# An encoder block on one core: the beginning ordered by hand with all loads ahead of the stores, norm weights spread by transpositions, TensorE and GpSimd by hand in branch B, meta keys as one block

## Chip, core and metric

The kernel runs on one core of a Trainium2 chip. Its time is the device time in microseconds (us) of one execution. Engines: PE (TensorE), PEld (its weight loads), DVE (VectorE), ACT (ScalarE), POOL (GpSimd), SP (the engine that issues the DMAs).

## What is computed

1024 tokens of width 1024, with 16 meta tokens put ahead, go through one block; all is fp32.

```python
h = concat(meta, x)                                  # 1040 x 1024
proj = rms_norm(h, norm_mix) @ w_in                  # qa, ka, va, qb, kb, vb, gates
y_a = differential_attention(qa, ka, va)             # branch A: 4 heads of 2 x 64, all keys
y_b = windowed_gqa(qb, kb, vb, sink)                 # branch B: 8 heads, 2 groups of 4; keys of
                                                     # the own block of 128, both neighbours, meta
h = h + (sigmoid(ga) * (y_a @ w_ba) + sigmoid(gb) * (y_b @ w_bb)) @ w_o
h = h + (silu(f @ w_gate) * (f @ w_up)) @ w_down     # f = rms_norm(h, norm_ffn)
out = rms_norm(h, norm_final)[16:]
```

## The kernel before

Every fp32 operand is split in two fp32r tiles, hi and lo (`split`, L117 on ACT for hi, L118 on POOL or DVE for lo), and every product is three matmuls: hi·hi, hi·lo, lo·hi.

**Beginning.** Nine tiles of tokens (eight of 128, one of 16 meta tokens) are loaded (L383), squared on ACT (L134), given their factor on POOL (L122, L123), scaled by it and by the norm weights `gmix` on DVE (L140, `xn_a`), transposed on PE (L148, `ptn_a`) and split (L150, L151) into `hT_hi`, `hT_lo`, the transposed activations. `gmix` comes as a broadcast transfer of 128x1024 (L415). Warm-up matmuls on zeros (`idle`, L413, L426) stand ahead. Between the tiles, `advance` puts projection steps (L214; one step is the three matmuls of one of 8 row blocks) of KB and of two column blocks of QB, in chunks of 256 tokens. Their results are spread into `kb` and `qb` by 72 DMAs on SP (L282, L285, L305).

**Branch B.** VB is projected and transposed. There are 16 units, g = 0, 1 by t = 0 to 7. A unit has for each of its four heads r two score matmuls (`bps`, L331), on DVE bias and minimum (L333), on ACT the exponential (L337); then the sink's exponential (L339), denominators on DVE (L340, L341), four normalisations on POOL (L343), and a POOL copy `bmd` (L347) of the meta keys' probabilities, padded to 128 columns per head. `finish` transposes each block of keys, four heads each (L356, `bpt`), the meta block as a fourth one, splits the result (L358 ACT, L360 DVE, `btr`) and multiplies it with the values (L362, `bpy`); L365 to L367 store it. Units at the edges have two blocks of keys (288 columns), the others three (432). Beside the units with g = 0 run the projections of branch A's heads 0 and 1 (`project_a`: QA, VA, KA) and, on POOL, the token sums (L525 to L539, split on ACT and DVE as `to`); beside g = 1 heads 2 and 3 and the weight sums (L608 to L611).

**Order.** The scheduler orders each engine's queue by a simulated timeline, except inside `tc.manual_schedule`, where an engine keeps the order of the code. Before, POOL is by hand from the second QB projection on, PE from branch A on (L883). Branch A (`aps`, L796), gate products (`pg`, L717, L737), output projection, FFN (`pg`, L1293; `pd`, L1387) follow.

## Time and profile before

| | us |
|---|---|
| median of three runs | 1449.07 (1446.01, 1449.07, 1449.72) |
| the profiled execution | 1446.1 |
| its span, first to last instruction | 1444.3 |
| PE busy | 1422.8 |
| DVE, ACT, POOL busy | 899.2, 679.6, 641.3 |

Rows give the start or the stretch, the duration, the engine, the line and the tiles. Busy PE counts each matmul to its modelled end, which overlaps the start of the next.

### The profile page before, as it was taken

To read this page: it belongs to the slowest core of one execution; us is meant where nothing else is said; L and a number is where in the kernel's file an instruction comes from. 1 tells how busy PE (TensorE), PEld (TensorE's weight loads), DVE (VectorE), ACT (ScalarE), POOL (GpSimd) and SP (SyncE) were. 2 spreads that over 40 slices of the span, in tenths; PEclk is the share of its full clock that TensorE was granted. 3 is DMA by queue.
4 is the path that set the end of the run, shared out by engine and by line. 5 is a ranking of instruction groups with operands and counts; after the bars stand their busy time and mean duration, and the time that the engine had idled before them with its cause. 6 is when DMAs were issued, how large, how long until landed. Compare 5 with 4: busy or idle time off the path is not lost.

```text
span 1444.3 us, 21160 instructions
## 1 busy us (share of the span) xinstructions
PE 1422.8 (99%) x7279; PEld 1221.2 (85%) x7279; DVE 899.2 (62%) x1624; ACT 679.6 (47%) x1290; POOL 641.3 (44%) x605
## 2 busy tenths in 40 slices
...
GB/s 244 90 209 237 193 162 265 288 281 213 190 169 257 147 227 125 190 256 209 216 34 88 152 104 161 109 102 110 102 102 96 110 102 102 331 208 140 124 129 139
DMA packets 188891, 242.41 MB, mean 168 GB/s; under 512 B 18208, under 2 KB 115936, under 8 KB 188784
## 3 DMA queue, kind: packets, MB, share of 16 engines
...
q8 instruction: 57, 0.93, 0.3%
q14 instruction: 50, 0.41, 0.1%
...
## 4 chain that ended last, share of the span: by engine, by line
PE 81%; POOL 6%; DVE 5%; issue 4%; DMA 2%; ACT 1%; POOLq 0%; SPq 0%; DVEq 0%; ACTq 0%
PE pg L1293 28%; PE pd L1387 9%; PE pg L737 7%; PE po L1070 6%; PE ppa L780 6%; PE aps L796 3%; PE pp_qb L214 3%; POOL oa L118 3%; PE apy L835 3%; PE pp_ka L214 2%; PE pp_va L214 2%; PE apt L822 2%; PE pp_qa L214 2%; PE bpt L356 1%; PE bpy L362 1%
## 5 line engine op out<-in xcount | busy, mean ns | idle before, releaser
L118 POOL TENSOR_TENSOR wop<-wf,wop 128x512 fp32r<-128x512 f32 x128 | 172.6, 1353 | 165.5 <-ACT wop L117 149.6
L1293 PE MATMUL pg<-t,wop 128*128 128x512 f32 x1056 | 242.6, 389 | 0.0
L1293 PEld LDWEIGHTS pg<-t,wop 128*128 128x128 f32 x1056 | 198.3, 188 | 41.1
L1387 PE MATMUL pd<-ob,oa 128*128 128x512 f32 x924 | 209.9, 389 | 0.4 <-POOL oa L118 0.4
L1387 PEld LDWEIGHTS pd<-ob,oa 128*128 128x128 f32 x924 | 173.4, 188 | 36.8 <-POOL oa L118 0.8
L1293 PE MATMUL pg<-b,wop 128*128 128x512 f32 x792 | 185.6, 392 | 2.3 <-DVE c L1302 2.3
L1293 PEld LDWEIGHTS pg<-b,wop 128*128 128x128 f32 x792 | 149.5, 189 | 34.1 <-issue 2.4
L737 PE MATMUL pg<-hT_hi,gop 128*128 128x512 f32 x384 | 142.7, 396 | 0.0
L118 POOL TENSOR_TENSOR oa<-ra,oa 128x512 fp32r<-128x512 f32 x33 | 44.0, 1335 | 170.1 <-ACT oa L117 168.6
L117 ACT ACTIVATE wop<-wf 128x512 fp32r<-128x512 f32 x128 | 80.2, 631 | 82.9 <-PE pg L1293 48.6
L118 POOL TENSOR_TENSOR gop<-gr,gop 128x512 fp32r<-128x512 f32 x48 | 63.3, 1319 | 116.4 <-ACT gop L117 102.6
L117 ACT ACTIVATE oa<-ra 128x512 fp32r<-128x512 f32 x77 | 48.7, 632 | 105.9 <-PE pd L1387 45.1
L804 ACT ACTIVATE as<-as,amn 128x1040 f32<-128x1040 f32 x64 | 74.5, 1164 | 46.9 <-DVE amn L799 42.8
L1128 DVE TENSOR_TENSOR s<-wf,wf 128x512 f32<-128x512 f32 x22 | 25.0, 1138 | 108.1 <-DMA wf<-in_w_ff_gate_dram 58.0
L796 PE MATMUL aps<-ak,aq 128*128 128x392 f32 (+1 forms) x384 | 90.0, 330 | 1.3 <-DVE amn L799 0.6
L1070 PE MATMUL po<-woh,mT 128*128 128x512 f32 x384 | 88.0, 390 | 0.0
L1070 PEld LDWEIGHTS po<-woh,mT 128*128 128x128 f32 x384 | 71.9, 188 | 14.8
L796 PEld LDWEIGHTS aps<-ak,aq 128*128 128x128 f32 x384 | 69.6, 189 | 15.0 <-DVE amn L799 2.2
L737 PEld LDWEIGHTS pg<-hT_hi,gop 128*128 128x128 f32 x384 | 72.7, 189 | 11.2 <-DVE gk L742 0.2
L343 POOL TENSOR_SCALAR bs<-bs,bdn 128x432 f32<-128x432 f32 (+1 forms) x64 | 41.4, 666 | 85.5 <-DVE bdn L341 73.4
L737 PE MATMUL pg<-hT_lo,gop 128*128 128x512 f32 x192 | 76.0, 396 | 0.0
L807 POOL TENSOR_SCALAR as<-as,adn,neglam 128x1040 f32<-128x1040 f32 x32 | 38.8, 1214 | 62.5 <-DVE adn L805 43.9
...
## 6 DMA issues: line engine op xcount, KB each, us to landing
...
```

The source lines that it names most:

```text
L117: nc.scalar.activation(hi, src, AF.Copy)
L118: lo_eng.tensor_tensor(lo, src, f32(hi), ALU.subtract)
L214: nc.tensor.matmul(ps[:, :n], a[:, c, :], b[:, c, at:at + n], start=(c == 0 and i == 0), stop=(c == DC - 1 and i == 2))
L343: nc.gpsimd.tensor_scalar(st[:, r, :W], st[:, r, :W], dn[:, r:r + 1], 1.0, ALU.mult, ALU.mult)
L737: nc.tensor.matmul(ps, op[:, a, c], quad(b, *act)[:, c], start=(p in (2, 5, 1) and c == 0 and i == 0), stop=(p in (2, 3, 4) and c == 3 and ...
L780: nc.tensor.matmul(ps, w[:, a, j, :], src(j, b, tk), start=(j == 0 and n == 0), stop=(j == 3 and n == 2))
L796: nc.tensor.matmul(ps[:, :n], qs[m][:, t * P:(t + 1) * P], ks[m][:, vv, k0:k0 + n], start=(vv == 0), stop=(vv == 1))
L804: nc.scalar.activation(s[m][:, 0:L], s[m][:, 0:L], AF.Exp, bias=low, scale=-1.0, accum_out=dn[:, m:m + 1])
L835: nc.tensor.matmul(py[:, cols], v[:kp, a, k, :], at_[:kp, k, b, :], start=(k == 0 and j == 0), stop=(k == 8))
L1070: nc.tensor.matmul(ps, mT[:, c, a, t * P:(t + 1) * P], wos[q, c][:, b], start=(c == 0 and n == 0), stop=(c == DC - 1 and n == 2))
L1293: nc.tensor.matmul(ps, op[:, x, c, :], b[:, y, c, :], start=(p in (1, 2, 5) and c == 0 and n == 0), stop=(p in (4, 2, 3) and c == 3 and n ...
L1387: nc.tensor.matmul(ps[u], oa[:, a, u * P:(u + 1) * P], ob[:, b, :], start=(p in (1, 2, 5) and j == 0 and k == 0), stop=(p in (2, 3, 4) and ...
```

## The change

- **Beginning.** All engines keep the order of the code until tile 6 is turned. The loads of x and of the weights of KB and QB are issued before the first store. The norm weights come as 8x128, are transposed, and eight transposes of a broadcast column build `gmix`. Warm-ups are 24 instead of 22. The first two KB chunks multiply all hi·hi first, then hi·lo, then lo·hi.
- **Branch B.** PE (from VB on) and POOL keep the order of the code. A unit is cut in two generators, `scores()` (a step per head; the last also issues the normalisation) and `turns()` (meta transpose and first block; a block each; values and store). `plan` hangs them on projection steps: scores at base-14, -12, -10, -8, turns at base, +4, +8, +12, with base = 16t+4 for g = 0 and 182+13t for g = 1; a piece of the token sums every 8 steps.
- **Meta keys.** The probabilities of four heads by 32 columns (each meta key twice) are one 128x128 block with one transpose. Four ACT copies and four DVE subtractions put it block-diagonally into `diag`, against values with the meta rows repeated eight times.
- **Small.** One tile for the small loads; `vb1` allocated later; one Silu activation after the merging, so that the table is loaded there.

PE around unit 2 of g = 0 (`bps_2_3` are its last scores; `va`, `qa` are branch A's projections; `bpt_2_8` the meta transpose). Before:

```order
L331 MATMUL bps_2_3_1103<-kb_146,qb_156 128x432 x2
L362 MATMUL bpy_0_1053<-btr_0_0_1059,vb_148 128x512
...
L356 MATMUL bpt_1_8_1151<-ident,bmd_151 128x128 x3
L356 MATMUL bpt_2_1_1198<-ident,bs_2_1087 128x128 x4
...
L356 MATMUL bpt_2_8_1228<-ident,bmd_150 128x128 x2
L362 MATMUL bpy_2_1197<-btr_2_3_1223,vb_148 128x512
```

70 rows lie between the scores and the unit's first transposes, and 140 between them and the meta transposes. Now, on the same engine:

```order
L348 MATMUL bps_2_3_1316<-kb_146,qb_149 128x432 x2
L225 MATMUL pp_va_384_1288<-hT_hi,wh_c_1063 128x384
...
L381 MATMUL bpy_1_1224<-btr_1_2_1311,vb_148 128x512 x2
L399 MATMUL bpy_1_1224<-diag,vb_148 128x512
L225 MATMUL pp_va_768_1358<-hT_hi,wh_c_1063 128x272
...
L385 MATMUL bpt_2_8_1372<-ident,bmd_2_1329 128x128
L374 MATMUL bpt_2_1_1376<-ident,bs_2_1257 128x128 x4
```

The meta transpose comes first of the transposes, behind 12 matmuls of 384 columns (four steps), three `bpy` and 12 of 272.

ACT at the same unit (`to` are splits of token sums, which POOL computes; `bes` the sink's exponentials). Before:

```order
L337 ACTIVATE bs_2_1087,bdn_2_1089<-bs_2_1087,bmn_2_1088 128x432
L117 ACTIVATE to_1_1619<-ta_1_1614 128x512
L337 ACTIVATE bs_2_1087,bdn_2_1089<-bs_2_1087,bmn_2_1088 128x432 x2
L339 ACTIVATE bes_2_1090<-bes_2_1090 128x4
L358 ACTIVATE btr_0_8_1079<-bpt_0_8_1074 128x512
```

Now:

```order
L117 ACTIVATE to_0_1186<-ta_0_1181 128x512
L352 ACTIVATE bs_2_1257,bdn_2_1259<-bs_2_1257,bmn_2_1258 128x432 x2
L376 ACTIVATE btr_1_2_1311<-bpt_1_2_1306 128x512
L352 ACTIVATE bs_2_1257,bdn_2_1259<-bs_2_1257,bmn_2_1258 128x432
L117 ACTIVATE to_0_1250<-ta_0_1182 128x512
L357 ACTIVATE bes_2_1260<-bes_2_1260 128x4
```

A second `to` stands between the last exponential and that of the sink.

The beginning on SP. Before:

```order
L383 DMA x_185<-in_x_dram 128x1024
L415 DMA gmix<-in_norm_mix_dram 128x1024
L383 DMA x_188<-in_x_dram 128x1024
L180 DMA w_c_190<-in_w_in_dram 128x8x128
L383 DMA x_203<-in_x_dram 128x1024
```

Now:

```order
L459 DMA g_168<-in_norm_mix_dram 8x128
L421 DMA x_170<-in_x_dram 128x1024
L421 DMA x_172<-in_x_dram 128x1024
L178 DMA w_174<-in_w_in_dram 128x8x128
L178 DMA w_176<-in_w_in_dram 128x8x128
L421 DMA x_178<-in_x_dram 128x1024
```

The norm weights are 4 KB instead of 512 KB and stand ahead of tile 0. The diff, cut to its core:

```diff
+            dots = [(c, i) for c in range(DC) for i in range(3)]
+            if name == "kb" and at < 512:
+                dots.sort(key=lambda d: d[1])
             for c in range(DC):
-                for i, (a, b) in enumerate(terms):
-                    nc.tensor.matmul(ps[:, :n], a[:, c, :], b[:, c, at:at + n],
-                                     start=(c == 0 and i == 0), stop=(c == DC - 1 and i == 2))
+                for d, i in dots[3 * c:3 * c + 3]:
+                    a, b = terms[i]
+                    nc.tensor.matmul(ps[:, :n], a[:, d, :], b[:, d, at:at + n],
+                                     start=((d, i) == dots[0]), stop=((d, i) == dots[-1]))
...
+        meta = vt[:, S:S + 2 * NM]
+        if name == "vb":
+            meta = bpool.tile([P, P], F32, tag="by1", name="vb_meta", bufs=2)
+            nc.vector.tensor_copy(meta.rearrange("p (a k) -> p a k", a=8), vt[:, S:L].unsqueeze(1).broadcast_to([P, 8, NM]))
...
+            for r in range(4):
+                ps = bank(psum1, "bs", f"bps_{nm}_{r}", 2)
+                for v in range(2):
+                    nc.tensor.matmul(ps[:, :W], qb[:, r, t * P:(t + 1) * P],
+                                     kb[g][:, v, b0:b1, :].rearrange("p b k -> p (b k)"), start=(v == 0), stop=(v == 1))
+                nc.vector.tensor_tensor_reduce(st[:, r, :W], ps[:, :W], tb, 2.0 ** -(4 * g + r + 1), nsink[:, 4 * g + r:4 * g + r + 1],
+                                               ALU.add, ALU.min, mn[:, r:r + 1])
+                nc.scalar.activation(st[:, r, :W], st[:, r, :W], AF.Exp, bias=mn[:, r:r + 1], scale=-1.0,
+                                     accum_out=dn[:, r:r + 1])
+                if r < 3:
+                    yield
+            nc.vector.tensor_tensor(es, mn, sinkb[:, 4 * g:4 * g + 4], ALU.add)
+            nc.scalar.activation(es, es, AF.Exp)
+            nc.vector.tensor_tensor(dn, dn, es, ALU.add)
+            nc.vector.reciprocal(dn, dn)
+            for r in range(4):
+                nc.gpsimd.tensor_scalar(st[:, r, :W], st[:, r, :W], dn[:, r:r + 1], 1.0, ALU.mult, ALU.mult)
+            md = held["md"] = bpool.tile([P, 4, 2, NM], F32, tag="bmd", name=f"bmd_{nm}", bufs=2)
+            nc.gpsimd.tensor_copy(md, st[:, :, own:own + NM].unsqueeze(2).broadcast_to([P, 4, 2, NM]))
+            yield
+
+        def turns():
+            st, md, dg, trs = held["st"], held["md"], diag[:, t % 2], {}
             py = bank(psum1, "by", f"bpy_{nm}", 1)
-            blocks = [(k, P, (k - b0) * 144) for k in range(b0, b1)] + [(8, P, (t - b0) * 144 + P)]
-            for k, kp, o in blocks:
+
+            def turn(k):
+                o = (k - b0) * 144
                 pt = bank(psum1, "bt", f"bpt_{nm}_{k}", 2).rearrange("p (r t) -> p r t", r=4)
                 for r in range(4):
-                    nc.tensor.transpose(pt[:kp, r, :], st[:, r, o:o + P] if k < 8 else md[:, r], ident)
-                tr = bpool.tile([P, 2, 4, P], F32R, tag="btr", name=f"btr_{nm}_{k}", bufs=4)
-                nc.scalar.activation(tr[:kp, 0], pt[:kp], AF.Copy)
-                lo = tr[:, 1] if k < 8 else tr[:NM, 0]
-                nc.vector.tensor_tensor(lo, pt[:lo.shape[0]], f32(tr[:lo.shape[0], 0]), ALU.subtract)
-                for hl in range(2 if k < 8 else 1):
-                    nc.tensor.matmul(py, vb[g][:kp, k, :], tr[:kp, hl].rearrange("p r t -> p (r t)"),
-                                     start=(k == b0 and hl == 0), stop=(k == 8))
+                    nc.tensor.transpose(pt[:, r, :], st[:, r, o:o + P], ident)
+                tr = trs[k] = bpool.tile([P, 2, 4, P], F32R, tag="btr", name=f"btr_{nm}_{k}", bufs=4)
+                nc.scalar.activation(tr[:, 0], pt, AF.Copy)
+                nc.vector.tensor_tensor(tr[:, 1], pt, f32(tr[:, 0]), ALU.subtract)
+
+            def value(k):
+                for hl in range(2):
+                    nc.tensor.matmul(py, vb[g][:, k, :], trs[k][:, hl].rearrange("p r t -> p (r t)"),
+                                     start=(k == b0 and hl == 0), stop=False)
+
+            pt = bank(psum1, "bt", f"bpt_{nm}_8", 2)[:, 0:P]
+            nc.tensor.transpose(pt, md.rearrange("p r a k -> p (r a k)"), ident)
+            sc = bpool.tile([P, P], F32, tag="bsc", name=f"bsc_{nm}", bufs=2)
+            nc.scalar.copy(sc, pt)
+            turn(b0)
+            for r in range(4):
+                hi, lo = slice(32 * r, 32 * r + 32), slice(32 * r, 32 * r + NM)
+                nc.scalar.activation(dg[hi, r], sc[hi], AF.Copy)
+                nc.vector.tensor_tensor(dg[lo, r], sc[lo], f32(dg[lo, r]), ALU.subtract)
+            yield
+            for k in range(b0 + 1, b1):
+                turn(k)
+                value(k - 1)
+                yield
+            value(b1 - 1)
+            nc.tensor.matmul(py, vb[g][:, 8, :], dg.rearrange("p r t -> p (r t)"), start=False, stop=True)
             y1 = bpool.tile([64, 512], F32, tag="by1", name=f"by1_{nm}", bufs=2)
             nc.scalar.copy(y1, py[64:128])
             nc.vector.tensor_tensor(y1, py[0:64], y1, ALU.add)
             nc.sync.dma_start(yb_d[g][:, t * P:(t + 1) * P].rearrange("(r p) s -> p r s", p=64),
                               y1.rearrange("p (r s) -> p r s", r=4))
-        return finish
+            yield
+
+        return scores(), turns()
...
+    xpool, close_xpool = pool("xpool", "right")
+    order_0 = tc.manual_schedule()
+    order_0.__enter__()
     zeros = bpool.tile([P, 512], BF16, tag="by1", name="zeros", bufs=2)
     nc.vector.memset(zeros, 0.0)
     idle = bank(psum1, "by", "idle", 1)
-    for _ in range(15):
-        nc.tensor.matmul(idle, zeros[:, 0:P], zeros, start=True, stop=True)
+
+    def warm(n):
+        for _ in range(n):
+            nc.tensor.matmul(idle, zeros[:, 0:P], zeros, start=True, stop=True)
+
+    g8 = bpool.tile([8, P], F32, tag="by1", name="g8", bufs=2)
+    nc.sync.dma_start(g8, norm_mix.rearrange("o (k d) -> (o k) d", k=8))
     load_x(0)
-    nc.sync.dma_start(gmix, norm_mix.broadcast_to([P, D]))
     load_x(1)
+    ask(C_KB)
+    ask(C_QB)
+    load_x(2)
+    ask(C_QB + P, bpool)
+    load_x(3)
+    for t in (4, 5, 6):
+        load_x(t, xpool)
+    warm(6)
+    gt8 = small.tile([P, 8], F32, name="gt8", bufs=1)
+    pt8 = pp_bank("pt_g8")[:, 0:8]
+    nc.tensor.transpose(pt8, g8, ident[:8, :8])
+    nc.vector.tensor_copy(gt8, pt8)
+    for b in range(2):
+        pf = pp_bank(f"pf_g{b}")
+        for c in range(4):
+            k = 4 * b + c
+            nc.tensor.transpose(pf[:, c * P:(c + 1) * P], gt8[:, k:k + 1].broadcast_to([P, P]), ident)
+        nc.vector.tensor_copy(gmix[:, 512 * b:512 * b + 512], pf)
+    warm(10)
+
+    def square(t):
+        i = len(done)
+        done.append(t)
+        p, tag, bufs = (vtpool, "vt", 1) if i % 3 == 2 else (bpool, "bs", 2)
+        xn = xns[t] = p.tile([P, D], F32, tag=tag, name=f"xn_a{t}", bufs=bufs)
+        ss = small.tile([P, 1], F32, tag="ss", name=f"ss_a{t}")
+        nc.scalar.activation(xn, xts[t], AF.Square, accum_out=ss)
+        factors[t] = rstd_of(ss, D, P, f"rstd_a{t}")
+
+    def scale_x(t):
+        nc.vector.scalar_tensor_tensor(xns[t], xts.pop(t), factors.pop(t), gmix, ALU.mult, ALU.mult)
+
+    factors = {}
+    square(0)
+    scale_x(0)
+    load_x(7)
+    square(1)
+    scale_x(1)
+    load_x(NT)
+    turn_x(0)
+    warm(4)
     ensure(1)
-    norm_x(0)
-    load_x(2)
-    norm_x(1)
-    xn0 = xns[0]
-    turn_x(0)
-    zeros = bpool.tile([P, 512], BF16, tag="by1", name="zeros", bufs=2)
-    nc.vector.tensor_scalar(zeros, xn0[:, 0:512], 0.0, None, ALU.mult)
-    for _ in range(7):
-        nc.tensor.matmul(idle, zeros[:, 0:P], zeros, start=True, stop=True)
+    turn_x(1)
+    warm(4)
+    p_kb = project_steps(C_KB, KB_CHUNKS, "kb", evac_split(None, kb_consume))
     ensure(2)
-    load_x(3)
-    norm_x(2)
-    turn_x(1)
-    p_kb = project_steps(C_KB, KB_CHUNKS, "kb", evac_split(None, kb_consume))
     p_q0 = qb_steps(0, qb, 0)
+    early += [(p_kb, DC), (p_q0, DC)]
+    square(2)
+    advance(DC)
+    scale_x(2)
+    prepped[C_QB + P] = prep(C_QB + P, "qbx", lowpool, nc.vector)
     p_q1 = qb_steps(0, qb, 1)
-    prepped[C_QB + P] = prep(C_QB + P, "qbx", lowpool, nc.vector)
+    square(3)
+    advance(DC)
+    scale_x(3)
+    turn_x(2)
+    square(4)
+    early += [(p_q1, DC)]
+    advance(6)
+    turn_x(3)
+    advance(2)
+    scale_x(4)
+    square(5)
     early += [(p_kb, DC), (p_q0, DC), (p_q1, DC)]
-    advance(E_STEPS)
-    norm_x(3)
-    turn_x(2)
-    advance(E_STEPS)
-    load_x(4)
-    norm_x(4)
-    turn_x(3)
-    early += [(p_kb, DC), (p_q0, DC), (p_q1, DC)]
-    advance(E_STEPS)
-    load_x(5)
-    norm_x(5)
+    advance(DC)
     turn_x(4)
-    advance(E_STEPS)
-    load_x(6)
-    load_x(NT)
-    norm_x(6)
+    scale_x(5)
+    advance(DC)
     turn_x(5)
-    early += [(p_kb, DC), (p_q0, DC), (p_q1, DC)]
-    advance(E_STEPS)
-    load_x(7)
+    square(6)
+    scale_x(6)
+    advance(DC)
+    turn_x(6)
+    order_0.__exit__(None, None, None)
+    close_xpool()
...
+    order_pe = tc.manual_schedule(engines={mybir.EngineType.PE})
+    order_pe.__enter__()
+    order_pool = tc.manual_schedule(engines={mybir.EngineType.Pool})
+    order_pool.__enter__()
+    diag = bpool.tile([P, 2, 4, P], F32R, tag="bys", name="diag", bufs=1)
+    nc.gpsimd.memset(f32(diag), 0.0)
+    tiles_b = {(0, t): attend_b(0, t, qb) for t in range(NT)}
+    for i, _ in enumerate(stream_v(C_VB, "vb", vb_evac)):
+        if i in (12, 14, 16, 18):
+            next(tiles_b[0, 0][0])
...
+    at_step, events, extras = [0], {}, {}
+
+    def plan(g, t, base, scores=True):
+        sc, tu = tiles_b[g, t]
+        for i in range(4 if scores else 0):
+            events.setdefault(base - 14 + 2 * i, []).append(sc)
+        for i in range(4 if 0 < t < NT - 1 else 3):
+            events.setdefault(base + 4 * i, []).append(tu)
+
+    def along(steps):
+        for _ in steps:
+            at_step[0] += 1
+            for what in events.pop(at_step[0], ()):
+                next(what, None)
+            if at_step[0] in extras:
+                extras.pop(at_step[0])()
...
-    units_b(0, qb, first_b)
-    for c in range(2):
-        token_sums(c)
-    project_a(0)
-    token_sums(2)
-    project_a(1)
-    token_sums(3)
+    for t in range(NT):
+        plan(0, t, 16 * t + 4, t > 0)
+    pieces = [token_sums(c) for c in range(4)]
+    for n in range(16):
+        extras[8 * n + 5] = lambda g=pieces[n // 4]: next(g, None)
+    along(project_a(0))
+    along(project_a(1))
...
-    units_b(1, qb, extra=sums_of)
+    for t in range(NT):
+        tiles_b[1, t] = attend_b(1, t, qb)
+        plan(1, t, 182 + 13 * t)
+        extras[182 + 13 * t - 7] = lambda t=t: sums_of(t)
+    along(project_a(2))
+    along(project_a(3))
+    assert not events and not extras, (events, extras)
...
+    silu = small.tile([P, 1], F32, tag="silu", name="silu", bufs=1)
+    nc.scalar.activation(silu, gt[:, 0:1], AF.Silu)
```

124 lines of the change are left out of this document (48 added, 76 removed).

## The prediction

> **What bounds the kernel now.** I read the page first: its header with the span, the busy shares, and the chain of work that ended last.
>
> ```profile
> span 1444.3 us, 21160 instructions
> PE 1422.8 (99%) x7279; PEld 1221.2 (85%) x7279; DVE 899.2 (62%) x1624; ACT 679.6 (47%) x1290; POOL 641.3 (44%) x605
> PE 81%; POOL 6%; DVE 5%; issue 4%; DMA 2%; ACT 1%; POOLq 0%; SPq 0%; DVEq 0%; ACTq 0%
> ```
>
> TensorE is busy 1422.8 of 1444.3 us, so a change here can pay in two ways only: fewer TensorE instructions, or fewer of the 21.5 us in which it stood. The second view shows where these lie: busy time by stretch (span of the stretch, then PE, PEld, DVE, ACT, POOL, granted clock, DMA share, GB/s). The third is PE's waits, with their totals in us, their count and the longest.
>
> ```profile
> 12.80:56.00 43.20, 41.29 (x344) 40.37 (x345) 33.70 (x51) 23.62 (x45) 29.75 (x29) 1.00 0.62 164
> 56.00:73.30 17.30, 16.31 (x102) 15.02 (x102) 5.94 (x24) 7.23 (x24) 2.54 (x2) 1.00 0.41 81
> 73.30:325.70 252.40, 252.21 (x1440) 227.74 (x1440) 143.09 (x301) 131.11 (x293) 154.04 (x193) 1.00 0.77 234
> ```
> ```profile
> PE ptn_a L148 <- DVE xn_a L140: 2.8, 2, 1.9
> PE pg L1293 <- DVE c L1302: 2.3, 2, 2.0
> PE pp_qb L214 <- DVE wb_qbx L118: 1.5, 1, 1.5
> PE idle L413 <- DVE zeros L410: 1.2, 1, 1.2
> PE bps L331 <- DVE bmn L333: 1.0, 3, 0.5
> ```
>
> From 73.3 to 325.7 us, in which all but the first scores of branch B run, TensorE stands 0.2 us. **That is the key row**: a new order of TensorE has nothing to win in that stretch and can only lose there. What can be won lies ahead of 73.3 us, and in the transpositions that are saved.
>
> **Part 1: TensorE's own work.** The transposes and the warm-up, as start, duration and count:
>
> ```profile
> 276.90 0.38 PE L356 MATMUL bpt<-ident,bs 128*128 128x128 f32 x2
> 277.36 0.82 PE L356 MATMUL bpt<-ident,bs 128*128 128x128 f32 x6
> 8.82 1.67 PE L426 MATMUL idle<-zeros 128*128 128x512 bf16 x7
> ```
>
> Six against two transposes last 0.44 us longer, so one more takes TensorE 0.11 us. Each of the 16 units has three fewer (one of the meta block in place of four): 48 x 0.11 = 5.3 us less. The spread of the norm weights adds 9 of them (+1.0), and there are 24 warm-up matmuls instead of 22 (1.67 / 7 = 0.24 each, +0.5). Work: **-3.8 us**. The additions for ScalarE and VectorE, per unit a copy of 128x128, four of 32x128 and four subtractions of 16x128 in place of one 128x512 copy and one 16x512 subtraction, lie on engines that are 62% and 47% busy; they come between the meta transpose and its value matmul, which is the last of the unit, 8 to 12 projection steps later.
>
> **Part 2: the beginning.** From the chain (start, duration, what) and the timeline:
>
> ```profile
> 1.63 6.17 DMA x<-in_x_dram
> 47.56 3.02 PE pp_kb L214 x24
> 50.58 5.65 PE pp_qb L214 x48
> 56.23 7.35 PE pp_vb L214 x42
> ```
> ```profile
> 4.43 1.06 ACT L134 ACTIVATE xn_a<-x 128x1024 f32<-128x1024 f32 x1 [2.43 <-DMA x<-in_x_dram]
> 10.10 1.28 DVE L140 SCALAR_TENSOR_TENSOR xn_a<-x,rstd_a,gmix 128x1024 f32<-128x1024 f32 x1
> 11.43 1.10 PE L148 MATMUL ptn_a<-ident,xn_a 128*128 128x128 f32 x8 [0.93 <-DVE xn_a L140]
> 12.78 0.38 PE L214 MATMUL pp_kb<-hT_hi,wh_c 128*128 128x256 f32 x1 [0.25 <-ACT hT_hi L150]
> ```
>
> Ahead of the first matmul of VB (56.2) stand 264 projection matmuls of 256 columns (5.65 / 48 = 0.118 each), 24 of 272 (0.126), 72 transposes (0.11, the last eight narrower) and 22 warm-ups: 31.1 + 3.0 + 7.6 + 5.2 = 46.9 us. So 9.3 us are lost by then, 5.8 of them before the first projection matmul at 12.78 (7.0 us of work), and the rest mostly in the two longer waits above (xn_a 2.8 in two, wb_qbx 1.5). The norm weights come as a 512 KB transfer between tile 0 of x (landed at 4.43) and tile 1 (landed at 7.80, where the chain's DMA piece ends): two transfers of 512 KB in 3.4 us, 1.7 each. Without it tile 1 lands about 1.7 us earlier, less the tiny transfer put ahead of all (0.4); the steps behind it (1.06 of ScalarE for the squares, 1.28 of VectorE for xn, the transposes) keep their durations. Walked through: x_0 at 4.85, x_1 at 6.5, the KB weights at 8.2, first projection matmul at 11.9, which is 0.9 sooner with 1.5 us more work ahead of it. Lost until then: 3.4 instead of 5.8. Of the 3.5 lost later, the 1.5 for wb_qbx should go, since its split now stands directly behind the normalising of tile 2; but VectorE has 33.7 of 43.2 us in this stretch and its order is now fixed, so I give back half of it and keep 2.8. Lost at the beginning: 6.2 instead of 9.3, **-3.1 us**. Bounds: 0 (VectorE, not the loads, sets the pace) and -5.
>
> From 56.0 to 73.3 the view shows 1.0 us of standing, but busy time counts the ends of matmuls that nothing follows. By work there are VB's 48 matmuls of 384 columns (7.35 / 42 = 0.175) and 24 of 272, nine transposes, 16 score matmuls (some 0.13 and 0.2) and two of QB: 8.4 + 3.0 + 1.0 + 2.6 + 0.2 = 15.2 of 17.3 us, so 2.1 are lost, all where bps waits for VectorE at the end. The first unit's scores now stand two projection steps apart (six matmuls, 1.05 us, against some 0.7 of VectorE each) and the second unit's lie among QA's steps, so this goes: **-2.1 us**.
>
> **Part 3: what the order by hand costs in branch B.** TensorE now meets the meta transpose of a unit a fixed number of instructions behind the unit's last scores. Between the two lies a chain over three engines. Three units of before show it: last score pair on TensorE, denominators on VectorE, four normalisations and the meta copy on GpSimd.
>
> ```profile
> 274.37 0.56 PE L331 MATMUL bps<-kb,qb 128*128 128x432 f32 x2
> 276.55 0.16 DVE L340 TENSOR_TENSOR bdn<-bdn,bes 128x4 f32<-128x4 f32 x1 [0.71 <-ACT bes L339]
> 277.12 2.43 POOL L343 TENSOR_SCALAR bs<-bs,bdn 128x432 f32<-128x432 f32 x4 [2.33 <-PE bpy L362]
> 279.62 0.29 POOL L347 COPY bmd<-bs 128x128 f32<-128x128 f32 x1
> ```
> ```profile
> 237.14 0.54 PE L331 MATMUL bps<-kb,qb 128*128 128x432 f32 x2
> 242.78 0.29 POOL L347 COPY bmd<-bs 128x128 f32<-128x128 f32 x1
> ```
> ```profile
> 260.56 0.96 PE L331 MATMUL bps<-kb,qb 128*128 128x432 f32 x4
> 267.67 0.29 POOL L347 COPY bmd<-bs 128x128 f32<-128x128 f32 x1
> ```
>
> The chain took 279.91 - 274.37 = 5.5 us with the engines free for it, 243.07 - 237.14 = 5.9 with GpSimd busy on sums, and 267.96 - 260.95 = 7.0 (the last pair starts two 0.195 us matmuls into that row) with a projection's split on VectorE and a late exponential. The edge units, 288 columns wide, take about 0.65 less. Against it stands the work that TensorE has between. For unit 2 of g = 0, by the rows of TensorE shown with the change: the pair (0.39), 12 matmuls of 384 columns (2.1), three of 512 (0.7), 12 of 272 (1.5), together 4.7 us. The 16 units the same way: 5.9, 5.2, 4.7, 5.7, 5.4, 5.9, 4.7, 5.6 for g = 0; 5.2, 5.2, 7.0, 5.9, 7.9, 6.7, 5.8, 5.4 for g = 1. TensorE waits for the difference where it is positive. Summed: 2.3 us by the chain of 5.5, 4.7 by 5.9, 18 by 7.0. Before, the row of the window's transposes came some 70 rows behind the scores, which is why nothing was lost. I take 5.9, the middle row, in which GpSimd has other work, as it will have: **+4.7 us**, in some eight waits of at most 1.2 us.
>
> **Part 4: the rest.** Only the activation that brings the Silu table forward remains.
>
> ```profile
> 818.63 1.28 ACT L1304 ACT_TABLE_LOAD   x1
> ```
>
> VectorE is busy without a break from 812 to 833, where the wait of pg for c (2.0 us) ends, so 1.3 us taken from ScalarE's queue at 818.6 move nothing: 0, at best -1.3. Everything else behind 325.7 keeps its order on every engine.
>
> **Sum.** -3.8 - 3.1 - 2.1 + 4.7 = -4.3 us against the profiled execution's 1446.1 (its span of 1444.3 and 1.8 around it): 1441.8. That execution is the quickest of the three shown; on the median's scale (1449.07) the same difference gives 1444.8. I put down 1442.5. A measurement of this kernel can tell about 0.3%, 4.3 us, from no change, so the likeliest case lies right on that bound.
>
> **The rivals.**
> *Slower: the chain in branch B decides.* ScalarE's order now has the splits of the token sums, which wait for GpSimd, ahead of the exponentials of units 2, 4 and 6; VectorE has the matching subtraction ahead of the denominators. GpSimd in turn has two pieces of the token sums, some five additions, and mostly a weight split between the normalisations of two units.
>
> ```profile
> L530 POOL TENSOR_TENSOR ta<-hT_hi 128x512 f32<-128x512 f32 x4 | 6.1, 1516 | 0.0
> ```
> ```profile
> 10.97 2.64 POOL L118 TENSOR_TENSOR wl_c<-w_c,wh_c 128x1024 fp32r<-128x1024 f32 x1 [1.07 <-ACT wh_c L117]
> ```
>
> Five additions (7.6 us), a split (2.6) and normalising (2.7) make 12.9 us, and a unit of 16 steps takes TensorE 12 to 16. If the chain is 7.0 us, the third row, all along, the waits sum to 18 and the time is 1446.1 - 9.0 + 18 = 1455; at 6.3 us the gain is used up. For it: a late start anywhere in three in-order queues lengthens the chain, and TensorE no longer works around it. Against it: two of three rows are below 6.3, and in g = 1 the token sums are gone and the lags longer.
> The clock could add to it:
>
> ```profile
> 22.00:24.50 2.50, 0.97 (x9) 0.77 (x8) 2.50 (x4) 1.99 (x5) 0.98 (x2) 1.00 0.99 291
> 337.00:341.00 4.00, 2.97 (x13) 2.71 (x14) 3.85 (x11) 3.68 (x8) 2.29 (x2) 0.71 1.05 407
> 834.00:838.00 4.00, 4.00 (x13) 3.12 (x13) 4.00 (x7) 1.02 (x3) 0.00 (x0) 0.63 0.08 26
> ```
>
> After the 1.5 us wait for wb_qbx the granted clock stayed 1.00; after the 2.0 us wait for c it fell to 0.63 for 4 us, 1.5 us of work lost. In my forecast no wait reaches 2 us; by a chain of 7.0 two do (2.3 us at units 2 and 6), 3 us more: 1458. [...]
> *The same: the beginning gains nothing.* VectorE, 33.7 of 43.2 us busy, sets its pace and VB still starts at 56: 1446.1 - 4.3 + 3.1 = 1444.9. For it: the waits named are all for VectorE. Against: several steps are moved out of its way.
> *Faster than forecast: the cover holds.* With the chain of 5.5 and the beginning at its better bound: -3.8 - 5 - 2.1 + 2.3 = -8.6, 1437.5.
> *It doesn't do what it says*, i.e. ScalarE and VectorE, still ordered by the scheduler, put a unit's steps elsewhere: their rows stand at the unit's place, so this has nothing left but the slower rival.
>
> **How the numbers follow.** Forecast 0.42 (it straddles the bound: 0.26 faster, 0.16 same); cover holds 0.20 (faster); beginning gains nothing 0.13 (0.03 faster, 0.10 same); chain decides 0.25 (0.06 same, 0.19 slower). Faster 0.49, same 0.32, slower 0.19. The range reaches from 1435 (both better bounds and the table load) to 1453, short of the slower rival's full price, about 0.1 on either side left out.
>
> **What would show it.** Work right: 192 transposes bpt. Beginning right: first projection matmul at 11 to 12.5, first of VB at 54 to 55; wrong if at 56. Branch B right: waits of bpt for GpSimd's bmd totalling 3 to 7 us, none above 1.5, and the first aps at 320 to 323 instead of 325.7. Wrong if those waits pass 9 us, if a window in branch B has a clock below 1.00, or if bps waits for DMA or VectorE instead.

## The result and the profile after

The changed kernel takes **1490.47 us** (median of four runs, 1488.26 to 1492.86), the kernel before 1449.39 beside it: ratio **1.0288 [1.0265, 1.0311]**, 41 us slower. The prediction was 1442.5, its range 1435 to 1453. The profiled execution took 1490.68.

The head of its page, with the clock of the 40 slices:

```profile
span 1488.9 us, 21131 instructions
PE 1434.5 (96%) x7242; PEld 1221.4 (82%) x7242; DVE 932.5 (63%) x1676; ACT 698.0 (47%) x1355; POOL 634.6 (43%) x602
PEclk9989999999999999999999999999999999999999
```

TensorE has fewer instructions and yet 44.6 us more of span. Where they arise is seen by the first score matmul of branch A, which stood at 325.7 us before:

```profile
L899 PE MATMUL aps<-ak,aq x60: 276/340/445, 366.7 to 399.4; 128*128 128x392 f32 x40, 128*128 128x256 f32 x20
```

It stands at 366.7: 41.0 of the 44.6 us come ahead of it, the last 3.6 behind. The first projection matmul started at 11.99 and the first of VB at 56.41, so the 41 lie in branch B. Its stretches (first of before, then of after; PE, PEld, DVE, ACT and POOL busy with their instruction counts, granted clock, DMA share, GB/s):

```profile
73.30:85.00 11.70, 11.70 (x57) 9.70 (x57) 6.77 (x17) 6.74 (x16) 10.49 (x13) 1.00 0.87 273
85.00:205.00 120.00, 119.81 (x688) 108.51 (x687) 73.46 (x139) 61.15 (x134) 64.28 (x62) 1.00 0.67 196
```

```profile
73.30:85.00 11.70, 4.49 (x16) 3.63 (x17) 0.79 (x3) 1.53 (x3) 7.73 (x8) 0.56 0.34 95
85.00:205.00 120.00, 103.53 (x559) 91.84 (x559) 87.17 (x164) 67.69 (x168) 74.00 (x76) 0.96 0.47 147
```

From 73 to 85 TensorE does 4.5 us of work in 11.7, and the clock falls to 0.56. From 85 to 205 it does 129 matmuls fewer in the same time. VectorE has 13.7 us more to do there, by only 25 instructions more. What TensorE waited for, by the view of waits (total us, times, longest):

```profile
PE bpt L385 <- POOL bmd L363: 13.0, 11, 2.4
PE pp_qa L225 <- POOL wl_c L118: 8.3, 1, 8.3
PE bpy L381 <- DVE btr L377: 6.8, 8, 1.6
PE bps L348 <- DVE bmn L350: 4.0, 3, 1.6
```

With 1.5 of smaller ones that is 33.6 us, where before had 1.2. The rest of the 41 is longer busy time of TensorE. Busy time times what was missing of the clock gives some 6 us of it (4.49 x 0.44 + 103.53 x 0.04, an estimate).

Two of the four waits were in no part of the prediction. **The single one of 8.3 us**, in the timeline (start, duration, engine; in brackets the idle time before, and what ended it):

```profile
72.21 0.58 SPq L579 DMA_DIRECT2D few<-in_lambda_q_dram  x1
72.84 0.46 SPq L579 DMA_DIRECT2D few<-in_lambda_k_dram  x1
73.40 7.47 SPq L186 DMA_DIRECT2D w_c<-in_w_in_dram  x2
...
76.53 0.29 DVE L581 TENSOR_TENSOR lam_p<-few 128x128 f32<-128x128 f32 x1 [4.66 <-DMA few<-in_lambda_k_dram]
...
77.20 0.95 POOL L593 MEMSET diag<- 128x1024 f32 x1 [22.71 <-DVE lam_s L583]
...
78.12 2.34 POOL L118 TENSOR_TENSOR wl_c<-w_c,wh_c 128x1024 fp32r<-128x1024 f32 x1
...
80.51 0.79 PE L225 MATMUL pp_qa<-hT_hi,wl_c 128*128 128x512 f32 x1 [8.34 <-POOL wl_c L118]
```

`diag` shares its buffer with `lam_p`, so GpSimd's first instruction of branch B, the clearing of `diag`, waits until `lam_p` has been read. `lam_p` is made of the small vectors, whose loads SP issues behind the 72 stores of KB and QB, at 72 us; in the kernel before it issued them at 9 to 13 us, ahead of all stores. GpSimd, now kept in order, holds the split of QA's weights behind the clearing.

**VectorE's extra time** is in the subtraction that puts the meta block into `diag`. Its group, then a piece of the timeline (consecutive like instructions in one row):

```profile
L392 DVE TENSOR_TENSOR diag<-bsc,diag 16x128 fp32r<-16x128 f32 x64 | 53.7, 839 | 28.4 <-ACT diag L391 26.9
```

```profile
102.01 1.63 DVE L392 TENSOR_TENSOR diag<-bsc,diag 16x128 fp32r<-16x128 f32 x2 [1.30 <-ACT diag L391]
102.16 1.34 POOL L626 TENSOR_TENSOR ta<-hT_lo 128x512 f32<-128x512 f32 x1
...
104.40 3.01 DVE L392 TENSOR_TENSOR diag<-bsc,diag 16x128 fp32r<-16x128 f32 x2
...
104.82 2.43 POOL L118 TENSOR_TENSOR wl_c<-w_c,wh_c 128x1024 fp32r<-128x1024 f32 x1
```

An operation on 16x128 elements takes 839 ns on average; a 128x512 split takes 680. The second pair ends at 107.41, when GpSimd's 2.43 us instruction ends (107.25); the first ends at 103.64, GpSimd's at 103.50.

### The profile page after: what moved, and what is told of

Its sections match the earlier page's. It is cut to its first block, busy times and chain, and to the rows that moved or that the text cites. A ratio compares the mean times of both kernels' runs of the same rounds, so it can differ in the third digit from the quotient of the medians.

```text
span 1488.9 us, 21131 instructions
## 1 busy us (share of the span) xinstructions
PE 1434.5 (96%) x7242; PEld 1221.4 (82%) x7242; DVE 932.5 (63%) x1676; ACT 698.0 (47%) x1355; POOL 634.6 (43%) x602
## 4 chain that ended last, share of the span: by engine, by line
PE 67%; DVE 10%; issue 7%; POOL 6%; DMA 4%; ACT 4%; SPq 0%; POOLq 0%; DVEq 0%; ACTq 0%
PE pg L1396 27%; PE pd L1490 8%; PE pg L840 7%; PE ppa L883 6%; PE po L1173 5%; PE aps L899 3%; POOL oa L118 3%; PE apy L938 3%; DVE diag L392 2%; POOL bs L361 2%; PE pp_qb L225 2%; PE apt L925 2%; DVE bs L350 1%; PE pg L820 1%; DMA ak<-ka_d 1%
## 5 line engine op out<-in xcount | busy, mean ns | idle before, releaser
L361 POOL TENSOR_SCALAR bs<-bs,bdn 128x432 f32<-128x432 f32 (+1 forms) x64 | 38.1, 614 | 104.2 <-DVE bdn L359 77.4
L840 PEld LDWEIGHTS pg<-hT_hi,gop 128*128 128x128 f32 x384 | 72.2, 188 | 11.2 <-DVE gk L845 0.2
L392 DVE TENSOR_TENSOR diag<-bsc,diag 16x128 fp32r<-16x128 f32 x64 | 53.7, 839 | 28.4 <-ACT diag L391 26.9
```

The lines of the kernel that those rows point to most:

```text
L361: nc.gpsimd.tensor_scalar(st[:, r, :W], st[:, r, :W], dn[:, r:r + 1], 1.0, ALU.mult, ALU.mult)
L392: nc.vector.tensor_tensor(dg[lo, r], sc[lo], f32(dg[lo, r]), ALU.subtract)
L840: nc.tensor.matmul(ps, op[:, a, c], quad(b, *act)[:, c], start=(p in (2, 5, 1) and c == 0 and i == 0), stop=(p in (2, 3, 4) and c == 3 and ...
```

## The experiments

Times are medians in us; "before" is the kernel before, timed beside the run; "first aps" is the start of the first score matmul of branch A in the profiled execution, as above (325.7 before, 366.7 after).

| run | this | before | ratio | first aps |
|---|---|---|---|---|
| e1_diag_free | 1489.15 | 1448.33 | 1.0280 [1.0264, 1.0295] | 366.1 |
| e2_psum_lo | 1475.59 | 1448.33 | 1.0184 [1.0169, 1.0199] | 350.4 |
| e3_both | 1468.72 | 1448.33 | 1.0135 [1.0118, 1.0152] | 345.2 |
| e4_before_sbuf (one execution) | 1452.67 | 1448.33 | | 331.1 |
| e5_small_early | 1466.93 | 1449.08 | 1.0118 [1.0101, 1.0135] | 343.1 |
| e6_lead18 | 1459.59 | 1449.08 | 1.0072 [1.0051, 1.0093] | 339.3 |
| e7_old_meta | 1466.57 | 1449.08 | 1.0124 [1.0102, 1.0146] | 342.5 |
| e8_meta_alone | 1454.12 | 1449.08 | 1.0038 [1.0025, 1.0050] | 334.4 |
| e9_sched_b | 1466.71 | 1447.61 | 1.0128 [1.0112, 1.0145] | 342.9 |
| e10_no_silu | 1457.97 | 1447.61 | 1.0070 [1.0055, 1.0086] | 333.9 |
| e11_begin_alone | 1452.03 | 1447.61 | 1.0029 [1.0018, 1.0041] | 324.2 |
| e12_pool_sched | 1484.74 | 1447.61 | 1.0258 [1.0241, 1.0275] | 362.5 |
| e13_begin_layout | 1447.87 | 1448.41 | 0.9994 [0.9985, 1.0002] | 324.1 |
| e14_all_mended | 1456.40 | 1448.41 | 1.0055 [1.0040, 1.0070] | 336.1 |
| e15_after_layout | 1487.33 | 1448.41 | 1.0263 [1.0247, 1.0279] | 366.5 |
| e16_before_pad32 | 1453.89 | 1448.41 | 1.0036 [1.0022, 1.0050] | 326.2 |

One of the four executions of e15 took 6543.63 us and is left out of its ratio; without it the median is 1486.33. What happened in it is not known.

### Which of the two: the held GpSimd, or the slow subtraction?

Theory A: the 8.3 us behind the clearing of `diag` are the largest single cost. Theory B: the subtraction reads two tiles in SBUF and is held while GpSimd works, and its 53.7 us delay everything in VectorE's queue. e1 gives `lam_p` another buffer; e2 takes the subtrahend from PSUM, where TensorE's transpose left it; e3 does both.

```diff
-    lam_p = bpool.tile([P, 2, HD], F32, tag="bys", name="lam_p", bufs=1)
+    lam_p = bpool.tile([P, 2, HD], F32, tag="btr", name="lam_p", bufs=4)    # e1, e3
...
-                nc.vector.tensor_tensor(dg[lo, r], sc[lo], f32(dg[lo, r]), ALU.subtract)
+                nc.vector.tensor_tensor(dg[lo, r], pt[lo], f32(dg[lo, r]), ALU.subtract)    # e2, e3
```

> Changed kernel, with lam_p in another buffer, so that clearing diag on GpSimd no longer waits for the lambda vectors. Theory A (the clearing stood ahead of the split of QA's weights and waited for four small transfers that SP issues behind its 72 stores): PE's wait of pp_qa for wl_c falls from 8.3 us to under 1.5, and with the clock lost behind it the time goes from 1490.5 to 1479 to 1482. Rival (PE would only wait for the next weights, which SP issues behind the same stores): less than 4 us, 1487 or more, and a new wait of pp_va for a weight split.

> Changed kernel, with the 64 subtractions into diag reading the transpose in PSUM instead of its copy in SBUF: one SBUF operand instead of two, same order by hand. Theory B (a VectorE instruction with two SBUF operands waits until the GpSimd instruction that runs has ended): their mean falls from 839 ns to under 250, waits of bpy for btr (6.8) and of bps for bmn (4.0) fall under 2 us in sum, those of bpt for bmd from 13.0 to about 8, time 1471 to 1477. Rival P (16 partitions at an odd offset are slow): still over 700 ns, time 1488 to 1492. Rival C (the lead of the scores is too short by itself, the subtractions do no harm): under 250 ns, but less than 5 us gained.

> Both edits. If A and B are independent their gains add: 1460 to 1468. If one hides the other (PE waits for the next thing in the queue), 1470 or more. What is left over before (1449) would then be the waits for bmd and the clock after them.

e1's two changed waits:

```profile
PE bps L348 <- DVE bmn L350: 8.1, 5, 3.6
...
PE bpt L374 <- ACT bsc L387: 2.0, 1, 2.0
```

The wait for `wl_c` is gone, but the time is not: some 1 us was won, which is within the noise. The time is the rival's, the way is not: no wait for VA's weights appeared. VectorE's queue stands at the same load (its `lam_p` multiplication still began at 77.24 us), so TensorE waits for VectorE's minima instead. As its own cause, A falls.

e2's group and its waits:

```profile
L392 DVE TENSOR_TENSOR diag<-bpt,diag 16x128 fp32r<-16x128 f32 x64 | 18.3, 286 | 27.5 <-ACT diag L391 25.7
```

```profile
PE bpt L385 <- POOL bmd L363: 11.1, 10, 2.4
PE pp_qa L225 <- POOL wl_c L118: 8.1, 1, 8.1
PE bpy L381 <- DVE btr L377: 2.7, 4, 1.2
```

839 ns become 286, the waits for VectorE shrink from 6.8 and 4.0 us to 2.7 and none, and the kernel is **15 us** faster (1490.47 to 1475.59; first aps 366.7 to 350.4). The time is the one that was expected, while 286 ns, 2.7 us and 11.1 us of waits for `bmd` are each somewhat above the expectation. B is shown. The clock between 85 and 205 us is 1.00, but it does not explain the gain: it is 1.00 there in e15 below as well, which keeps the slow subtraction, and first aps stands at 366.5 in e15.

With the subtraction mended, freeing `diag` is worth 7 us (e3 against e2), not 1: what a wait cost depended on what stood behind it. The time of e3, 1468.72, lies between the two that were expected.

The counter-test puts the same pattern into the kernel **before**: the meta block's subtraction, which read PSUM, reads a copy in SBUF.

```diff
-                nc.vector.tensor_tensor(lo, pt[:lo.shape[0]], f32(tr[:lo.shape[0], 0]), ALU.subtract)
+                src = pt
+                if k == 8:
+                    src = bpool.tile([NM, 4, P], F32, tag="by1", name=f"bsrc_{nm}", bufs=2)
+                    nc.scalar.copy(src, pt[:NM])
+                nc.vector.tensor_tensor(lo, src[:lo.shape[0]], f32(tr[:lo.shape[0], 0]), ALU.subtract)
```

> Kernel before, with the one subtraction of 16x512 per unit for the meta keys (680 ns there, reading PSUM and SBUF) reading an SBUF copy of the transpose: two SBUF operands. Theory B: its mean rises to 1.0 us or more while GpSimd works, by up to a GpSimd instruction (1.3 us beside the token sums, 0.7 beside normalisations and weight sums); PE does not wait for it, so the time stays at 1446 to 1451. Rival P: the duration stays at 0.68 us or below.

The group in before, and in e4:

```profile
L360 DVE TENSOR_TENSOR btr<-bpt,btr 16x512 fp32r<-16x512 f32 x16 | 10.8, 672 | 8.2 <-ACT btr L358 8.1
```

```profile
L364 DVE TENSOR_TENSOR btr<-bsrc,btr 16x512 fp32r<-16x512 f32 x16 | 15.9, 992 | 14.4 <-ACT bsrc L363 14.4
```

Same shape, same engine, 672 ns with one operand in SBUF and 992 with two (up to 2039). The time of its one execution, 1452.67, is above the 1446 to 1451 that was expected. The ends of the two pairs above, and both runs, agree with theory B. In the trace of the changed kernel 55 of the 64 subtractions took more than 0.3 us (up to 2.37), and each of these ended 0.14 to 0.16 us after a GpSimd instruction had ended; the other nine took 0.27 to 0.29. With one operand in PSUM (e2) the longest of the 64 took 0.30.

### The small loads behind the stores

e5 is e2 with the six small loads issued on SP right behind the meta tokens, ahead of every store, in another buffer (`by1`).

```diff
     load_x(NT)
+    few = bpool.tile([P, 5, HD], F32, tag="by1", name="few", bufs=2)
+    nc.sync.dma_start(few[:, 4, 0:1], subln.rearrange("o p -> p o"), allow_slow_non_contiguous=True)
+    nc.sync.dma_start(few[:, 4, 8:8 + BH], sink.broadcast_to([P, BH]))
+    for i, v in enumerate((lq1, lk1, lq2, lk2)):
+        nc.sync.dma_start(few[:, i, :], v.broadcast_to([P, HD]))
...
```

> Changed kernel with the PSUM subtraction, and the six small loads (lambda vectors, sinks, gain) issued on SP right behind the meta tokens, ahead of the stores, as before the change; diag and lam_p share their buffer as in the change. Theory A (what held GpSimd, VectorE and ScalarE until 77 us was a wait for these loads, in three queues): the 8.1 us wait for wl_c and the 3.0 us wait of bpt for btr that replaced it both go, 1461 to 1467. Rival (the weights for VA, issued at 73.4 us behind the same stores, are late too): a wait of pp_va for a weight split of 2 us or more, and 1468 or above.

The waits left in branch B:

```profile
PE bpt L385 <- POOL bmd L363: 11.1, 10, 2.4
PE bpy L381 <- DVE btr L377: 2.7, 4, 1.2
PE bpt L374 <- DVE btr L377: 2.0, 2, 1.4
PE pp_qa L225 <- DVE vb L308: 1.2, 1, 1.2
```

The 8.1 us are gone, and the time fell by 8.7 to 1466.93, as expected. The clock from 56 to 85 us is 1.00 (0.84 in e2). So small loads that were late in SP's queue cost some 9 us. e5 is the base of the next runs.

### The chain that the order by hand has to wait for

e5's largest wait is the one the prediction priced: TensorE at the meta transpose. The longest of them, from the last score pair on:

```profile
129.97 0.55 PE L348 MATMUL bps<-kb,qb 128*128 128x432 f32 x2
...
130.51 0.67 DVE L118 TENSOR_TENSOR to<-ta,to 128x512 fp32r<-128x512 f32 x1
...
131.11 0.65 DVE L350 CUSTOM_DVE_ANT_0 bs<-bps,tbx,nsink 128x432 f32<-128x432 f32 x1
...
132.46 1.05 ACT L117 ACTIVATE wh_c<-w_c 128x1024 fp32r<-128x1024 f32 x1
133.68 0.19 ACT L357 ACTIVATE bes<-bes 128x4 f32<-128x4 f32 x1
...
135.12 0.16 DVE L359 RECIPROCAL bdn<-bdn 128x4 f32<-128x4 f32 x1
135.48 2.42 POOL L361 TENSOR_SCALAR bs<-bs,bdn 128x432 f32<-128x432 f32 x4 [6.23 <-DVE bdn L359]
137.97 0.29 POOL L363 COPY bmd<-bs 128x128 f32<-128x128 f32 x1
```

From the end of the scores (130.52) to the copy's end (138.26) it is 7.7 us, and TensorE stands for 2.37 of them. In between, VectorE does a split of the token sums (0.67) first, ScalarE a split of the weights (1.05) ahead of the sink's exponential, and GpSimd sits idle for 6.23. Does a longer lead help, and by all of it? e6 hangs the scores four steps earlier, at base-18 (and pads the tile of the small activation, to no effect).

```diff
-            events.setdefault(base - 14 + 2 * i, []).append(sc)
+            events.setdefault(base - 18 + 2 * i, []).append(sc)
```

> As the run with early small loads, with the scores four projection steps earlier (base-18 instead of base-14; about 2.1 to 2.8 us of lead more), and the silu tile padded so that the small pool grows by 64 bytes instead of 36. Theory C (the chain from the last scores to bmd takes 7 to 8 us in the queues and is longer than the lead): waits of bpt for bmd fall from 10 us to under 3, and the time by 7 to 11 against the run before it. Rival (the queues of ScalarE and VectorE are what is full, more lead only moves the wait): waits of bps or bpy rise instead, less than 4 us gained. For the FFN's gate stage, which takes 427 to 428 us in all kernels of the changed family and 425 before at the same clock: if the shift of addresses by 36 bytes is the cause, 425 to 426.

```profile
PE bpt L374 <- DVE btr L377: 5.8, 6, 1.7
PE bpy L381 <- ACT btr L376: 2.2, 1, 2.2
PE pg L820 <- POOL wl_c L118: 1.7, 1, 1.7
```

All ten waits for `bmd` are gone and the kernel is **7.3 us** faster, not 11.1: in their place TensorE waits for splits of the transposed blocks and of weights, in the same queues of VectorE, ScalarE and GpSimd. In this execution the sum of the waits in branch B is 13.1 us, against 17.0 in e5, and the clock 0.97 from 85 to 205 us. Executions differ here by some us: e10 and e14, whose branch B is the same, have first aps at 333.9 and 336.1, waits of 11.0 and 11.2 and, in e10, a clock of 1.00. So the sizes of steps are taken from medians below, not from first aps.

Is it the order by hand at all? e9 leaves TensorE in all of branch B and GpSimd in g = 0 to the scheduler, e12 only GpSimd in g = 0.

```diff
-    order_pe = tc.manual_schedule(engines={mybir.EngineType.PE})    # e9 (entered behind branch B)
-    order_pe.__enter__()
-    order_pool = tc.manual_schedule(engines={mybir.EngineType.Pool})    # e9, e12 (entered ahead of g = 1)
-    order_pool.__enter__()
```

> As the run with early small loads (PSUM subtraction, one meta block), with the order of TensorE in branch B and of GpSimd in g = 0 left to the scheduler, as before the change. If the fixed order of TensorE is what costs the rest there, waits of bpt for bmd vanish, the first aps starts at 325 to 332 instead of 343, and the time is 1447 to 1455. Rival (the added work of the block and the new beginning cost it, whatever the order): 1460 or more.

> As the run with early small loads, with TensorE by hand but GpSimd in g = 0 left to the scheduler. If the pieces of the token sums put by hand between the normalisations are what makes the chain long, the waits of bpt for bmd fall from 11 us to 5 or less and the time to 1460. If it is the queues of ScalarE and VectorE, nothing much changes: 1463 to 1469.

e9's and e12's largest waits:

```profile
PE pg L818 <- POOL wl_c L118: 12.6, 1, 12.6
```

```profile
PE bpt L385 <- POOL bmd L363: 25.2, 10, 10.0
```

In e9 the waits for `bmd` vanish as the theory said, but the time is the rival's (1460 or more): one wait of 12.6 us, for a weight split that GpSimd reaches late, costs the same, and the total is that of e5 (1.0128 against 1.0118). GpSimd is by hand from g = 1 on, and its rows show what held the split:

```profile
327.04 0.20 POOL L769 MEMSET av<- 128x128 f32 x1 [8.91 <-DMA yb_d<-by]
...
330.19 2.34 POOL L118 TENSOR_TENSOR wl_c<-w_c,wh_c 128x1024 fp32r<-128x1024 f32 x1
```

It stands idle ahead of the clearing of a tile of branch A (`av`) until the last store of branch B has landed, with the split behind it: the same pattern as `diag` in the changed kernel. So e9 shows that the waits for `bmd` come from the order by hand; it does not show what another order of branch B could reach. In e12 both expectations missed: with TensorE by hand, GpSimd left to the scheduler makes the waits 25.2 us. Here at least, an engine held to an order needed its feeder held to one.

### The block of meta keys

e7 is e5 with four padded transposes and one wide split per unit, as before. e8 is the kernel before with the block alone (subtracted from PSUM).

```diff
...
-            nc.tensor.transpose(pt, md.rearrange("p r a k -> p (r a k)"), ident)
+            for r in range(4):
+                nc.tensor.transpose(pt[:, r, :], md[:, r], ident)
+            tm = bpool.tile([P, 4, P], F32R, tag="btm", name=f"btm_{nm}", bufs=1)
+            nc.scalar.activation(tm, pt, AF.Copy)
+            nc.vector.tensor_tensor(tm[:NM], pt[:NM], f32(tm[:NM]), ALU.subtract)
...
```

> As the run with early small loads, but with the meta keys as before the change: four padded transposes, one copy and one 16x512 subtraction from PSUM, no diag. Everything else by hand as in the change. If the block is a gain once it doesn't read SBUF twice, this is 3 to 6 us slower than that run (48 transposes more). If its nine small instructions per unit on ScalarE and VectorE lengthen the chain by as much as it saves, the two are within 3 us.

> Kernel before, with the meta keys as one block and nothing else (subtractions from PSUM, order left to the scheduler). If the 48 transposes are worth what one lasts (0.11 us) and the order still hides the rest: 1448.3 - 5.3, so 1442 to 1445. Rival (the added ScalarE and VectorE work or the one diag buffer per two units is waited for): 1447 or more.

e7's waits in branch B:

```profile
PE bpt L384 <- POOL md L360: 8.9, 9, 1.9
PE bpy L379 <- DVE btr L375: 2.9, 4, 1.3
PE pp_qa L225 <- DVE vb L305: 1.4, 1, 1.4
```

e5 and e7 tie (1466.93, 1466.57). The block does save TensorE 48 transposes, 5.3 us by the prediction, but e5's waits sum to 17.0 us where e7's sum to 13.2: 3.8 of the saved work come back as waits. The block puts nine small instructions per unit on ScalarE and VectorE, in place of two. Alone, on the kernel before (e8), it loses 5.0 us, as its rival said. Among its new waits are 2.8 us for `diag` and 5.6 for `wl_c`; the split for the latter stands behind the clearing of `av` again, ahead of which GpSimd is idle for 9.00 us. Whether the added instructions or only the changed order of the queues brought that about is not shown.

### The beginning, the Silu activation, and 32 bytes

e10 takes the Silu activation out of e6; e11 is the kernel before with the new beginning alone.

> As the run with scores four steps earlier, without the activation that brings the Silu table forward. If this activation is what makes the FFN's gate stage 427 to 428 us instead of 425, the stage falls by 2 to 3 and the time to 1457; if it is of no use and no harm, 1459 to 1460 and the stage stays.

> Kernel before with the change's beginning alone (loads ahead of stores, norm weights by transposes, order by hand until tile 6 is turned). My prediction's step: VB starts about 1.6 us sooner (3.1 less lost, 1.5 more work), 1446 to 1447.5. Rival (VectorE sets the pace, as in the changed kernel, where VB started at 56.4 instead of 56.2): 1448.5 to 1451.

e10 moved nothing beyond the noise. e11 missed both expectations: first aps came 1.5 us earlier (324.2), and yet the kernel was 4.4 us slower. The loss is behind it, in stages whose instructions are the same. The FFN's groups of 792 matmuls show it, in before, after and e11:

```profile
L1293 PE MATMUL pg<-b,wop 128*128 128x512 f32 x792 | 185.6, 392 | 2.3 <-DVE c L1302 2.3
```

```profile
L1396 PE MATMUL pg<-b,wop 128*128 128x512 f32 x792 | 187.6, 395 | 2.1 <-DVE c L1405 2.1
```

```profile
L1350 PE MATMUL pg<-b,wop 128*128 128x512 f32 x792 | 189.2, 396 | 1.7 <-DVE c L1359 1.7
```

Apart from the waits named there TensorE waits for nothing, and at clock 1.00 each matmul follows the last one a little later: 233.8 ns apart in e11, 229.5 in after, 226.6 in before (the typical run of n matmuls in the timeline, less one modelled duration of 389 ns, by n - 1). The totals of the groups show this less cleanly: in some executions, before and after among them, they hold one run at a lower clock, with some 301 ns. What e11 adds to the small pool, which lies below all later tiles, is a tile of 8 floats, `gt8`; every tile behind it moves up by 32 bytes. After adds that and the Silu tile of 4 bytes; e6, where this one is padded to 32 bytes, has the spacing of after and its 428 us for the stage, not the 425 to 426 that its expectation gave. e16 adds to the kernel **before** an unused tile of 32 bytes and its clearing, nothing else. e13 puts `gt8` of e11 into a tile that is there anyway; e14 does it to e6 without the Silu tile; e15 to the changed kernel itself, so that the addresses are before's.

```diff
+    pad = small.tile([P, 8], F32, name="pad", bufs=1)    # e16
+    nc.gpsimd.memset(pad, 0.0)
...
-    gt8 = small.tile([P, 8], F32, name="gt8", bufs=1)    # e13, e14, e15
+    start = bpool.tile([P, 512], F32, tag="by1", name="start", bufs=2)    # e13, e14, e15
+    zeros, gt8 = start[:, 0:256].bitcast(BF16), start[:, 256:264]
```

> The beginning alone, with gt8 (32 bytes, allocated in the small pool, which lies below all later tiles on the left) put into a tile that is there anyway, so that every later tile lies where it lay before the change. In the run of the beginning alone, matmuls of 512 columns in the FFN started every 233.8 ns (moving tile b) and 227.5 (t), against 226.6 and 226.6 in the kernel before, at the same granted clock and with no wait. Theory L (the addresses do this): both fall to 226.6, and the time to 1445.5 to 1447.5, 1.5 us below before, as VB's earlier start predicts. Rival (something else of the beginning): the spacings and 1452 stay.

> The changed kernel with all mends: subtraction from PSUM, small loads early, scores four steps earlier, no Silu activation, addresses as before the change. Theory L: FFN spacing 226.6 in both, 1453 to 1455.5 (1458.0 before this mend, less 3.6). What is left above 1448 are waits of branch B. Rival: 1457 or more.

> The changed kernel itself with nothing but the addresses put back (gt8 in an existing tile, silu tile and its activation left out). Theory L: FFN spacing 226.6, 1490.5 - 3.6 = 1487. Rival: 1489 to 1492.

> The kernel before with an unused tile of 32 bytes in the small pool and its clearing, nothing else. Theory L: the FFN's spacing rises to 233.8 (b) and 227.5 (t) as with the beginning alone, 1452 to 1456. Rival: 1447 to 1450.

The same group in e16 and e13:

```profile
L1295 PE MATMUL pg<-b,wop 128*128 128x512 f32 x792 | 189.2, 396 | 1.7 <-DVE c L1304 1.6
```

```profile
L1350 PE MATMUL pg<-b,wop 128*128 128x512 f32 x792 | 184.0, 390 | 2.3 <-DVE c L1359 2.3
```

e16's unused tile costs 5.5 us (1453.89 against 1448.41) and gives e11's spacing of 233.8, as expected; taken out of e11 (e13) the spacing is 226.6 again and the 4.4 us are gone (1447.87, just above what was expected). In e15 it is 226.6 as well, and the ratio falls from 1.0288 to 1.0263, some 3.6 us. The intervals of the two ratios overlap, but the place fits: from first aps to the end of the span it is 1117.9 us in e15, 1122.2 in after and 1118.6 in before. Which operand's address does it was not tried.

e14, with everything mended that was found, is at 1456.40, 1 us above its expectation, with a ratio of 1.0055: still 8 us slower than before. Its waits in branch B sum to 11.2 us (5.2 of `bpt` for the split `btr`, 1.7 for `wl_c`), and its first aps lags by 10.4. None of the versions beats the kernel before; the best, the beginning alone with the addresses kept, equals it.

## Why the prediction was wrong

Mended one after the other (after, e2, e5, e6, e14, before) the median goes 1490.5, 1475.6, 1466.9, 1459.6, 1456.4, 1448.4, with 2 us or so of doubt on each, the more as not all were measured on one chip. So the subtraction from two SBUF tiles cost 15 us, the late small loads 9, the chain beyond its lead 7, the addresses with the Silu tile 3, and 8 stay in e14, where the trace has 11.2 us of waits in branch B. The steps depend on each other (e1 against e3), so the shares hold for this order. Whether those last 8 us could be scheduled away is open; the one other order of both engines that was tried (e9) had a wait of its own.

- **Part 1, work -3.8: the failed step, and the largest.** It put the added copies and subtractions at nothing, because they "lie on" engines with time to spare, and showed no duration for any of them. In the pairs shown the subtraction lasted until GpSimd's instruction ended, 839 ns on average over all 64 instead of the 286 that it takes with one operand in PSUM (e2). It stands in VectorE's queue, through which all but one of the four large waits of TensorE in branch B run, and it cost 15 us (e2). The meta subtraction of the kernel before had one operand in PSUM (672 ns); the changed one has two in SBUF. Even with that mended, the kernel takes as long with the nine small instructions as with the transposes that they save (e5, e7).
- **Part 2, beginning -3.1 and score waits -2.1: gained at most 1.5.** First projection matmul at 11.99, as put down (11.9); first of VB at 56.41, not 54.6: for this step the rival that the beginning gains nothing was right. With TensorE's order in branch B left as it was, VB started no sooner either (56.5 in e11 and e13), and yet first aps came 1.5 us earlier: the waits of `bps` for `bmn`, 1.0 us in before, are gone there. In the changed kernel they rose to 4.0 us, and with the subtraction mended they are gone too (e2), so what undid this term was the subtraction. That the small loads go behind the stores, and that GpSimd's first instruction depends on them through a shared buffer, was not followed: it cost 9 us (e5).
- **Part 3, chain +4.7: right mechanism, wrong size.** The waits of `bpt` for `bmd` were 13.0 us, 11.1 with the subtraction mended, up to 2.4 each. The middle row of 5.9 us was taken, and 7.7 was measured at the longest wait of e5, where ScalarE and VectorE have splits ahead of the chain. The slower rival named these splits and the break-even (9.0 us of waits), so it had the mechanism; its 18 us of waits were too many and its price of 1455 was too low, since it kept the gains of parts 1 and 2. e5, which has 11.1 us of these waits, is at 1466.9. That e14 ends at 1456.4 does not bear the price out, for it has none of these waits.
- **The clock.** The prediction took a wait of 2.0 us as enough to lower the clock. That holds for some executions only. In the changed kernel the clock was 0.96 from 85 to 205 us: 1.00 up to 100 us, so it is no tail of the 8.3 us wait, and 0.89 from 110 to 120, where TensorE waits 2.17 us until 117.75. In e15 it was 1.00 over the same 120 us, with a wait of 2.15 us until 116.94: VA's matmuls of 272 columns, half of which run in that stretch, took 288 to 298 ns on average in e15 and 306 to 326 in the changed kernel. The wait for `c` was 2.0 us in before, e14, e13 and e15: in the 4 us behind it the clock was 0.63 and 0.64 in the first two and 1.00 in the others; the longest matmul of the group took 747 and 628 ns in the first two and 499 in the others. What decides it is not shown.
- **Part 4, the rest 0:** Silu is 0 (e10). But that everything else keeps its order did not mean that it keeps its time: some 3.6 us came from addresses. The prediction had said that a change can pay only by fewer instructions of TensorE or by less standing; the spacing of its matmuls is a third way, and it was not looked at.

What would show it wrong, the prediction said, were VB at 56, waits for `bmd` past 9 us, a clock below 1.00 in branch B, or waits of `bps` for VectorE: all four came (56.41, 13.0 us, 0.56 and 0.96, 4.0 us).
